# Two token tiles through a chain of feed-forward stages: one more weight unit of distance between the tiles, half of a mean square on VectorE, output stored in halves

## The chip, the cores and the metric

One core of one Trainium2 chip. The metric is the device time of one execution in microseconds; the kernel before has a median of 1438.19 us over 3 runs (1437.05 to 1443.36). PE is the matrix engine (TensorE), PEld its weight load, DVE is VectorE, ACT is ScalarE, POOL is GpSimd, SP issues the transfers.

## What is computed

256 tokens of width 1024 go through two blocks. The first block is a state-space mixer beside a sparse attention, merged, and then a feed-forward with a squared relu (width 4096). The second block has two layers, each with two gated feed-forwards (width 2816) around a mixer (retention in layer 0, latent attention in layer 1):

```python
def swiglu(h, w_gu, w_down):
    g, u = jnp.split(h @ w_gu, 2, axis=-1)
    return (jax.nn.silu(g) * u) @ w_down
...
        x = x + FFN_RES_WEIGHT * rms_norm(swiglu(rms_norm(x, ng[0]), ffn_w_gu[l, 0], ffn_w_down[l, 0]), ng[1])
        h = rms_norm(x, ng[2])
...
        x = x + rms_norm(mix, ng[3])
        x = x + FFN_RES_WEIGHT * rms_norm(swiglu(rms_norm(x, ng[4]), ffn_w_gu[l, 1], ffn_w_down[l, 1]), ng[5])
```

`rms_norm` divides by the root of the mean square over the 1024 columns and multiplies by a gain. So each branch's result is normalised once more before it is added to x; such an addition is called a gained residual below.

## The kernel before

The tokens are two tiles of 128, `t` = 0 and 1. x stays in SBUF, transposed, as `xT[t]` (128 x 8 x 128). Every product is made of three matmuls on values split into a high and a low part: `mm3` (L301) multiplies high by high, low weights by high, and high weights by low. Activations are split into `hTh`/`hTl` or `ffhh`/`ffhl`. Weights arrive in units of up to 128 x 2048 (1 MB) in a buffer `raw`; ACT casts a unit in four pieces to `wh` (L259), and DVE subtracts to get `wl` (L260). A unit is shared by the two tiles: it stays until both have used it, and only then can its buffers be filled again. There are 5 buffers of `wh` and `wl` each and 3 of `raw` in most of the stages here, 6 of `wh` and `wl` in the last one (`XB1`, `XB2`, L175 and L243 to L249).

The stages around the change are these. **f1**: `stage1` (up and down with 8 chunks of 512) and then the first gated feed-forward, ffn00 (11 chunks of 256). Then retention. **f2 of layer 0**: the output product of the mixer (`mix_out`, `wo`), its gained residual, ffn01, and then ffn10. Then latent attention. **f2 of layer 1**: `mix_out`, its gained residual, ffn11, and the output.

In a feed-forward (`ffn`, L423) a chunk's two up-products (12 matmuls for each unit and tile) go to a PSUM tile `mm`, ACT and DVE form `ffh` from it, PE transposes that (`tr`), ACT and DVE split it, and a down-product of 12 matmuls adds it to two accumulators of 512 columns (acc0, acc1 for tile 0; acc2, acc3 for tile 1). Each step of a tile's generator is one weight unit. `drive_gen` (L475) steps the two tiles by turns; tile 1 begins once tile 0 has done more steps than `lag`:

```python
            if alive[0]:
                step(0)
            if alive[1] and (pos[0] > lag or not alive[0]):
                step(1)
```

The default is `self.L`, 1. In f2 the generator of tile 0's `mix_out`, `W`, has already been stepped while the mixer ended, once in layer 0 and twice in layer 1, so tile 0 is there further ahead by that. A scheduler then orders each engine's instructions; what it makes of the steps is shown below as its order.

A residual (`resid`, L389) copies the accumulators to `tsb`, eight transposes on PE bring it back (`tr`), and DVE adds to `xT`. With a gain, ACT takes Square with an accumulated sum over each half (L400), DVE adds the two sums to `ms` (L402), POOL takes the power -1/2 (`rr`, L326), ACT scales the first half (L404) and DVE the second (L405), and DVE adds to `xT` in eight pieces (L420). There are 12 of these: two for ffn00, ffn01, ffn10, ffn11 and each of the two mixers. A stage starts with `norm`: eight pieces of `hTh` (ACT, L379) and `hTl` (DVE, L380), a Square on ACT, a reduction `s` on DVE (L365), and a one-column matmul with `ones`. Where tile 1's residual belongs to the next stage, it is kept in `left` and done there by `flush`.

At the end of `run` the two tiles of `xT` are stored, 512 KB each (L1260).

Of the kernel before, what the change touches and what calls it, by code (L numbers as in the profile page):

```python
# [12 lines left out]
AF = mybir.ActivationFunctionType  # L13
ALU = mybir.AluOpType
PSUM = bass.MemoryType.PSUM
P = 128
UW = 2048
EPS = 1e-6
# [159 lines left out]
class Prog:  # L178
# [207 lines left out]
            self.resid(pool, t, *self.left.pop(t), "sq")  # L386


    def resid(self, pool, t, acc, gain=None, tag=None):  # L389
        nc = self.nc  # L390
        xT = self.xT[t]
        if tag:
            tsb = self.sb(self.np, [P, 8, P], tag).rearrange("p c t -> p (c t)")
        else:
            tsb = self.sb(pool, [P, 1024], f"tsb{t}")
        if gain is not None:
            aa = self.sb(pool, [P, 2], "aa", bufs=4)
            for n in (0, 1):
                j = tsb[:, 512 * n:512 * n + 512]
                nc.scalar.activation(j, acc[n], AF.Square, scale=1.0 / 32.0, accum_out=aa[:, n:n + 1])  # L400
            ms = self.sb(pool, [P, 1], "ms", bufs=4)
            nc.vector.tensor_scalar(ms, aa[:, 0:1], aa[:, 1:2], EPS, op0=ALU.add, op1=ALU.add)  # L402
            r = self.rsqrt(pool, ms, 1, tag="rr")
            nc.scalar.mul(tsb[:, :512], acc[0], r)  # L404
            nc.vector.tensor_scalar_mul(tsb[:, 512:], acc[1], r)  # L405
        else:
            nc.scalar.copy(tsb[:, :512], acc[0])
            nc.vector.tensor_copy(tsb[:, 512:], acc[1])
        for h in (0, 1):
            pt = self.ps("tr")  # L410
            for c in range(4):
                cc = 4 * h + c
                self.tr(pt[:, c * P:(c + 1) * P], tsb[:, cc * P:(cc + 1) * P])
            if gain is None:
                v = xT[:, 4 * h:4 * h + 4, :].rearrange("p c t -> p (c t)")
                nc.vector.tensor_add(v, pt, v)
            else:
                for c in range(4):
                    cc = 4 * h + c
                    nc.vector.scalar_tensor_tensor(xT[:, cc, :], pt[:, c * P:(c + 1) * P], gain[:, cc:cc + 1], xT[:, cc, :], op0=ALU.mult, op1=ALU.add)  # L420


    def ffn(self, pool, t, hT, rstd, up, down, nch, width):  # L423
# [796 lines left out]
    def stage_ffn(self, pool, t, l, i, leave=False):  # L1220
        b = 3 + 6 * l + 4 * i
        h, r = self.norm(pool, t, self.gain(b))
        acc = yield from self.ffn(pool, t, h, r, f"gu{l}{i}", f"fd{l}{i}", 11, 256)
        gh = self.g05[:, 8 * (2 * l + i):8 * (2 * l + i) + 8]
        if leave:
            self.left[t] = (acc, gh)
        else:
            self.resid(pool, t, acc, gh)

    def run(self):  # L1230
        nc = self.nc
        self.consts()
        self.block1_mix()
        for l in (0, 1):
            for i in (0, 1):
                k = 2 * l + i
                nc.vector.tensor_scalar_mul(self.g05[:, 8 * k:8 * k + 8], self.gain(3 + 6 * l + 4 * i + 1), 0.5)
        self.dump("d_x0", self.xT[0])
        es0 = ExitStack()
        self.np = self.ctx.enter_context(self.tc.tile_pool(name="np", bufs=1))  # L1240
        mp = es0.enter_context(self.tc.tile_pool(name="mid", bufs=1))
        with ExitStack() as es:
            pool = es.enter_context(self.tc.tile_pool(name="f1", bufs=1))
            self.xp = es.enter_context(self.tc.tile_pool(name="f1x", bufs=1))
            self.un, self.XB = 0, XB1
            F = self.drive_gen([self.stage1(pool, 0), self.stage1(pool, 1)])
            for _ in range(12):
                next(F)
            D, M = self.decay(pool, mp), self.mem_prep(pool)
            for _ in D:  # L1250
                next(F)
            for _ in M:
                next(F)
            self.weave(F)
            self.xp = None
        self.layer_mix(0)
        es0.close()
        self.layer_mix(1)
        for t in (0, 1):
            nc.sync.dma_start(self.out[t], self.xT[t])  # L1260


    def attention(self, pool, heads, stags, otags):
# [61 lines left out]
    def layer_mix(self, l):  # L1325
        tc = self.tc
        with ExitStack() as es:
            with ExitStack() as es2:
                pool = es2.enter_context(tc.tile_pool(name=f"m{l}", bufs=1))
                self.xp = es2.enter_context(tc.tile_pool(name=f"m{l}x", bufs=1))  # L1330
                self.un, self.XB = 0, XBM[l]
                mix, W = (self.retention if l == 0 else self.mla)(pool)
                self.xp = None
            with ExitStack() as es2:
                pool = es2.enter_context(tc.tile_pool(name=f"f2{l}", bufs=1))

                def tail(t):
                    acc = yield from (W if t == 0 else self.mix_out(t, mix, f"wo{l}"))
                    self.resid(pool, t, acc, self.gain(3 + 6 * l + 3))
                    yield from self.stage_ffn(pool, t, l, 1)  # L1340
                    if l == 0:
                        yield from self.stage_ffn(pool, t, 1, 0, t == 1)

                self.xp = es2.enter_context(tc.tile_pool(name=f"f2{l}x", bufs=1))
                self.un, self.XB = 0, XB2[l]
                F = self.drive_gen([tail(0), tail(1)])
                if l == 0:
                    for _ in range(16):
                        next(F)
                    self.weave(F, self.mem_prep(pool))  # L1350
                self.weave(F)
                self.xp = None
# [277 lines left out]
```

## Time and profile before

| | |
|---|---|
| median of 3 runs | 1438.19 us |
| profiled execution | 1435.33 us, its span 1433.6 us |
| PE busy | 1383.9 us (97%) |
| PEld, DVE, ACT, POOL busy | 1111.8, 925.5, 754.2, 145.5 us |
| memory traffic | mean 166 GB/s |

The busy time of PE is counted from pipelined matmuls, so a busy PE is not a PE at its peak; a start-to-start distance of matmuls tells its pace. The feed-forward stages lie in the span as follows: stage1 from about 246 us, ffn00 from 438, f2 of layer 0 from 755 to about 1145 with ffn10 from 954, f2 of layer 1 from 1230 to the end. The granted clock is 1.00 (the upper of the two levels) in all slices of these stages but the last.

### The profile page before, as it was taken

The page shows a single profiled execution, that of the slowest core. Times are in us where ns is not written, and L with a number is a line of the kernel's source. Part 1 is how long each engine was busy: PE and PEld are TensorE (multiplying, and loading weights), DVE is VectorE, ACT ScalarE, POOL GpSimd, SP SyncE. Part 2 cuts the span into 40 slices and gives each one's busy share as a digit, 9 for nine tenths or more (in the row PEclk, how much of TensorE's full clock was granted, in tenths as well). Part 3 has the DMA queues.
Part 4 walks back from the last instruction along what each step waited for, and adds up shares of the span by engine and source line. Part 5 has one row for each costly group of instructions (what it writes and reads, how often), then busy time and mean ns, then how long its engine had stood idle before and what let it go on. Part 6 is the DMA issues. An engine that isn't in the chain of part 4 may idle for free.

```text
span 1433.6 us, 18512 instructions
## 1 busy us (share of the span) xinstructions
PE 1383.9 (97%) x6706; PEld 1111.8 (78%) x6706; DVE 925.5 (65%) x1970; ACT 754.2 (53%) x1650; POOL 145.5 (10%) x175
## 2 busy tenths in 40 slices
PE   7799899999999999999999999999999999999997
PEld 3466688788887888889887888878888887788886
DVE  6587667955667555577588565576555596765553
ACT  3246555644566444455367464465444576754442
POOL 3655200710000000012000000000000000000000
PEclk9899999999999999999999999999999999999999
DMA  9122255655564555435444555545555252555540
GB/s 345 67 89 78 89 178 176 244 200 176 177 209 170 179 180 195 147 100 191 142 172 168 197 210 179 198 153 206 176 190 192 78 182 78 185 206 186 195 147 30
DMA packets 38828, 238.64 MB, mean 166 GB/s; under 512 B 5712, under 2 KB 6992, under 8 KB 13136
## 3 DMA queue, kind: packets, MB, share of 16 engines
q1 hardware_dynamic: 38736, 237.45, 47.3%
q8 instruction: 53, 0.87, 0.2%
q14 instruction: 39, 0.32, 0.1%
HBM read 236.39 MB, written 1.05 MB: 166 GB/s over the span
## 4 chain that ended last, share of the span: by engine, by line
PE 77%; DVE 9%; POOL 5%; issue 4%; DMA 3%; ACT 2%; SPq 0%; POOLq 0%; DVEq 0%; ACTq 0%
PE mm L219 44%; PE acc L219 29%; PE tr L223 3%; DVE wl L260 2%; DMA raw<-in_wts_dram 2%; DVE s L365 1%; DVE hTl L380 1%; DVE xT L420 1%; POOL cst L719 1%; POOL cst L717 1%; PE tr L219 1%; DMA wl<-in_wts_dram 1%; ACT wh L259 1%; DVE tb L749 0%; POOL X L753 0%
## 5 line engine op out<-in xcount | busy, mean ns | idle before, releaser
L260 DVE TENSOR_TENSOR wl<-raw,wh 128x512 fp32r<-128x512 f32 (+2 forms) x860 | 539.9, 678 | 258.5 <-ACT wh L259 248.5
L259 ACT CAST wh<-raw 128x512 fp32r<-128x512 f32 (+2 forms) x860 | 466.2, 607 | 308.0 <-PE mm L219 158.7
L219 PE MATMUL mm<-wh,hTh 128*128 128x512 f32 (+1 forms) x1040 | 405.1, 390 | 8.5 <-DVE yn L1088 4.6
L219 PE MATMUL mm<-wh,hTl 128*128 128x512 f32 (+2 forms) x1072 | 412.3, 389 | 0.7 <-DVE hTl L380 0.7
L219 PE MATMUL mm<-wl,hTh 128*128 128x512 f32 (+1 forms) x1040 | 399.9, 385 | 0.0
L219 PEld LDWEIGHTS mm<-wh,hTl 128*128 128x128 f32 x1072 | 201.6, 188 | 44.5 <-issue 4.7
L219 PEld LDWEIGHTS mm<-wh,hTh 128*128 128x128 f32 x1040 | 195.7, 188 | 51.0 <-ACT hTh L379 5.8
L219 PEld LDWEIGHTS mm<-wl,hTh 128*128 128x128 f32 x1040 | 195.8, 188 | 37.0 <-issue 0.7
L219 PE MATMUL acc<-wh,ffhh 128*128 128x512 f32 x480 | 196.4, 409 | 0.0
L219 PE MATMUL acc<-wh,ffhl 128*128 128x512 f32 x480 | 188.9, 393 | 0.0
L219 PE MATMUL acc<-wl,ffhh 128*128 128x512 f32 x480 | 188.7, 393 | 0.0
L437 ACT ACTIVATE ffs<-mm,rstd 128x256 f32<-128x256 f32 x88 | 41.7, 474 | 135.8 <-PE mm L219 134.6
L438 DVE SCALAR_TENSOR_TENSOR ffh<-mm,rstd,ffs 128x256 f32<-128x256 f32 x88 | 42.4, 482 | 107.7 <-ACT ffs L437 105.7
L219 PEld LDWEIGHTS acc<-wh,ffhl 128*128 128x128 f32 x480 | 90.2, 188 | 20.2
L219 PEld LDWEIGHTS acc<-wl,ffhh 128*128 128x128 f32 x480 | 90.6, 189 | 16.8
L219 PEld LDWEIGHTS acc<-wh,ffhh 128*128 128x128 f32 x480 | 90.3, 188 | 16.5
L326 POOL TENSOR_TENSOR rr<-ms,mhalf 128x1 f32<-128x1 f32 x12 | 7.1, 595 | 780.5 <-DVE ms L402 780.5
L219 PE MATMUL acc<-wh,mx 128*128 128x512 f32 x160 | 53.9, 403 | 0.2 <-ACT wh L259 0.2
L319 ACT CAST ffhh<-tr 128x256 fp32r<-128x256 f32 (+1 forms) x104 | 41.7, 401 | 21.0 <-PE tr L223 21.0
L320 DVE TENSOR_TENSOR ffhl<-tr,ffhh 128x256 fp32r<-128x256 f32 (+1 forms) x104 | 47.6, 458 | 6.3 <-ACT ffhh L319 5.5
L223 PE MATMUL tr<-idn,ffh 128*128 128x128 f32 x240 | 43.2, 272 | 0.0
L223 PEld LDWEIGHTS tr<-idn,ffh 128*128 128x128 f32 x240 | 32.3, 140 | 13.3 <-DVE ffh L438 0.4
(403 smaller groups left out, 1372.2 us busy)
## 6 DMA issues: line engine op xcount, KB each, us to landing
raw<-in_wts_dram SPq DMA_DIRECT2D x195, 1024.0 KB, 4.9
raw<-in_wts_dram SPq DMA_DIRECT2D x18, 768.0 KB, 4.2
raw<-in_wts_dram SPq DMA_DIRECT2D x4, 576.0 KB, 3.5
wl<-in_wts_dram SPq DMA_DIRECT2D x2, 1024.0 KB, 6.8
g8k<-in_cw_dram SPq DMA_DIRECT2D x2, 1024.0 KB, 10.0
memT<-in_memT_dram SPq DMA_DIRECT2D x4, 512.0 KB, 4.1
raw<-in_wts_dram SPq DMA_DIRECT2D x4, 256.0 KB, 5.3
wh<-in_wts_dram SPq DMA_DIRECT2D x4, 256.0 KB, 7.4
```

The lines of the kernel that those rows point to most:

```text
L219: self.nc.tensor.matmul(out, l, r, start=start, stop=stop, **kw)
L223: self.nc.tensor.transpose(out, src, self.idn[:n, :n])
L259: self.copies[key] = nc.scalar.copy(wh[:, s:s + h], raw[:, s:s + h]).ins
L260: self.subs[key] = nc.vector.tensor_sub(wl[:, s:s + h], raw[:, s:s + h], wh[:, s:s + h].bitcast(F32)).ins
L319: self.nc.scalar.copy(hi, src)
L320: self.nc.vector.tensor_sub(lo, src, hi.bitcast(F32))
L365: nc.vector.tensor_reduce(s8, sq.rearrange("p c t -> p t c"), axis=mybir.AxisListType.X, op=ALU.add)
L380: nc.vector.scalar_tensor_tensor(lo[:, c, :], xT[:, c, :], g[:, c:c + 1], hi[:, c, :].bitcast(F32), op0=ALU.mult, op1=ALU.subtract)
L420: nc.vector.scalar_tensor_tensor(xT[:, cc, :], pt[:, c * P:(c + 1) * P], gain[:, cc:cc + 1], xT[:, cc, :], op0=ALU.mult, op1=ALU.add)
L437: nc.scalar.activation(s, pm[:, :256], AF.Silu, scale=rstd)
L438: nc.vector.scalar_tensor_tensor(h, pm[:, 256:], rstd, s, op0=ALU.mult, op1=ALU.mult)
L717: e.tensor_mul(C[n], A[0], B[n])
```

## The change

Three things are changed. The two drivers of feed-forward stages (f1 and f2) get a lag of 2 in place of 1. In a gained residual, ACT takes Square of the first half only; the second half's mean square is made on DVE from its mean and variance (`bn_stats`, `bn_aggr`, mean squared plus variance, halved, plus epsilon, plus the other half's sum). And in the last residual of each tile the four pieces of `xT` of each half are stored as soon as they are updated, 256 KB each, in place of the two stores at the end.

```diff
-    def resid(self, pool, t, acc, gain=None, tag=None):
+    def resid(self, pool, t, acc, gain=None, tag=None, out=False):
...
             aa = self.sb(pool, [P, 2], "aa", bufs=4)
-            for n in (0, 1):
-                j = tsb[:, 512 * n:512 * n + 512]
-                nc.scalar.activation(j, acc[n], AF.Square, scale=1.0 / 32.0, accum_out=aa[:, n:n + 1])
+            nc.scalar.activation(tsb[:, :512], acc[0], AF.Square, scale=1.0 / 32.0, accum_out=aa[:, 0:1])
+
+            bs, mv = self.sb(pool, [P, 6], "rbs", bufs=2), self.sb(pool, [P, 2], "rmv", bufs=2)
+            nc.vector.bn_stats(bs, acc[1])
+            nc.vector.bn_aggr(mv, bs)
             ms = self.sb(pool, [P, 1], "ms", bufs=4)
-            nc.vector.tensor_scalar(ms, aa[:, 0:1], aa[:, 1:2], EPS, op0=ALU.add, op1=ALU.add)
+            nc.vector.scalar_tensor_tensor(ms, mv[:, 0:1], mv[:, 0:1], mv[:, 1:2], op0=ALU.mult, op1=ALU.add)
+            nc.vector.tensor_scalar(ms, ms, 0.5, EPS, op0=ALU.mult, op1=ALU.add)
+            nc.vector.tensor_add(ms, ms, aa[:, 0:1])
             r = self.rsqrt(pool, ms, 1, tag="rr")
...
                     nc.vector.scalar_tensor_tensor(xT[:, cc, :], pt[:, c * P:(c + 1) * P], gain[:, cc:cc + 1], xT[:, cc, :], op0=ALU.mult, op1=ALU.add)
+                if out:
+                    nc.sync.dma_start(self.out[t][:, 4 * h:4 * h + 4], xT[:, 4 * h:4 * h + 4])
...
-            self.resid(pool, t, acc, gh)
+            self.resid(pool, t, acc, gh, out=l == 1 and i == 1)
...
-            F = self.drive_gen([self.stage1(pool, 0), self.stage1(pool, 1)])
+            F = self.drive_gen([self.stage1(pool, 0), self.stage1(pool, 1)], 2)
...
-        for t in (0, 1):
-            nc.sync.dma_start(self.out[t], self.xT[t])
...
-                F = self.drive_gen([tail(0), tail(1)])
+                F = self.drive_gen([tail(0), tail(1)], 2)
```

The order on the engines shows what becomes of it. First PE between `stage1` and ffn00, from the transposes of tile 1's residual on (`tsb1`; `hTh0` and `hTh1` are the two tiles' activations, and the first number behind a name counts its buffers). Before:

```order
L223 MATMUL tr_687_3878<-idn_1_67,tsb1_686_3875 128x128 x4
L223 MATMUL tr_688_3884<-idn_1_67,tsb1_686_3875 128x128 x4
L219 MATMUL mm_698_3920<-wh_681_3816,hTh1_689_3890 128x512
L219 MATMUL mm_698_3920<-wl_682_3817,hTh1_689_3890 128x512
L219 MATMUL mm_704_3944<-wh_706_3946,hTh0_670_3784 128x512
```

With the change:

```order
L223 MATMUL tr_696_3914<-idn_1_67,tsb1_695_3911 128x128 x4
L223 MATMUL tr_697_3920<-idn_1_67,tsb1_695_3911 128x128 x4
L219 MATMUL mm_691_3886<-wh_709_3970,hTh0_670_3772 128x512
L219 MATMUL mm_691_3886<-wl_710_3971,hTh0_670_3772 128x512
L219 MATMUL mm_691_3886<-wh_709_3970,hTl0_671_3773 128x512
L219 MATMUL mm_691_3886<-wh_709_3970,hTh0_670_3772 128x512
L219 MATMUL mm_707_3956<-wh_681_3804,hTh1_698_3926 128x512
```

Four matmuls of tile 0 now stand between the transposes and the first matmul of tile 1, whose operand `hTh1` is made from what those transposes bring; the 12 matmuls of tile 0's unit before that now stand ahead of the transposes.

Second, ACT in the middle of ffn11, between the casts of weight units (`wh`), the activations `ffs` and the splits `ffhh`. Before:

```order
L259 CAST wh_2077_11885<-raw_2076_11884 128x512 x4
L319 CAST ffhh_2069_11830<-tr_2068_11827 128x256
L259 CAST wh_2085_11932<-raw_2084_11931 128x512 x4
L259 CAST wh_2094_11980<-raw_2093_11979 128x512 x4
L437 ACTIVATE ffs_2080_11921<-mm_2071_11846,rstd01_1915_10908 128x256
L437 ACTIVATE ffs_2088_11956<-mm_2075_11871,rstd11_1949_11111 128x256
L319 CAST ffhh_2082_11927<-tr_2081_11924 128x256
```

With the change:

```order
L259 CAST wh_2117_12054<-raw_2116_12053 128x512 x4
L319 CAST ffhh_2114_12037<-tr_2113_12034 128x256
L259 CAST wh_2126_12102<-raw_2125_12101 128x512 x4
L443 ACTIVATE ffs_2121_12091<-mm_2107_12005,rstd01_1931_10939 128x256
L259 CAST wh_2130_12139<-raw_2129_12138 128x512
L319 CAST ffhh_2123_12097<-tr_2122_12094 128x256
L259 CAST wh_2130_12139<-raw_2129_12138 128x512 x3
```

The activations of the two tiles no longer follow each other; one unit's casts now stand between them, and one of its casts ahead of a split.

Third, DVE at the end of the program, from the last split on. Before:

```order
L320 TENSOR_TENSOR ffhl_2169_12459<-tr_2167_12455,ffhh_2168_12458 128x256
L402 TENSOR_SCALAR ms_2172_12490<-aa_2171_12487 128x1
L405 TENSOR_SCALAR tsb1_2170_12486<-acc3_1951_11114,rr1_2173_12492 128x512
L420 SCALAR_TENSOR_TENSOR xT1_6_79<-tr_2174_12496,g05_10_95,xT1_6_79 128x128 x4
L420 SCALAR_TENSOR_TENSOR xT1_6_79<-tr_2175_12505,g05_10_95,xT1_6_79 128x128 x4
```

With the change:

```order
L320 TENSOR_TENSOR ffhl_2191_12516<-tr_2189_12512,ffhh_2190_12515 128x256
L401 BN_STATS rbs_2194_12546<-acc3_1979_11199 128x6
L402 BN_AGGR rmv_2195_12547<-rbs_2194_12546 128x2
L404 SCALAR_TENSOR_TENSOR ms_2196_12550<-rmv_2195_12547 128x1
L405 TENSOR_SCALAR ms_2196_12550<-ms_2196_12550 128x1
L406 TENSOR_TENSOR ms_2196_12550<-ms_2196_12550,aa_2193_12544 128x1
L409 TENSOR_SCALAR tsb1_2192_12543<-acc3_1979_11199,rr1_2197_12554 128x512
L424 SCALAR_TENSOR_TENSOR xT1_6_79<-tr_2198_12558,g05_10_95,xT1_6_79 128x128 x4
L424 SCALAR_TENSOR_TENSOR xT1_6_79<-tr_2199_12568,g05_10_95,xT1_6_79 128x128 x4
```

Five operations stand where one stood ahead of the scaling by `rr`. In the order of the matmuls as a whole, ffn00 had 24 up-matmuls, 12 down-matmuls, 24 and 12 in turn and now has 48, 12 and 12; ffn11 had 48, 12 and 12 and now has 24, 12, 24 and 12; ffn01 and ffn10 have 48, 12 and 12 in both.

## Rows read from the trace of the kernel before

**Rows 1.** The page: span, then busy time, share and instructions of each engine.

```profile
span 1433.6 us, 18512 instructions
PE 1383.9 (97%) x6706; PEld 1111.8 (78%) x6706; DVE 925.5 (65%) x1970; ACT 754.2 (53%) x1650; POOL 145.5 (10%) x175
```

**Rows 2.** Busy time by stretch: PE, PEld, DVE, ACT, POOL, clock, DMA share, GB/s.

```profile
245.00:262.00 17.00, 15.01 (x73) 11.83 (x72) 16.90 (x30) 12.99 (x27) 1.82 (x2) 1.00 0.53 182
...
430.00:455.00 25.00, 22.77 (x108) 17.89 (x107) 21.31 (x42) 17.86 (x39) 1.48 (x2) 1.00 0.46 164
...
755.00:787.00 32.00, 31.06 (x145) 24.32 (x144) 27.08 (x63) 23.51 (x52) 2.94 (x4) 1.00 0.40 145
...
1230.00:1262.00 32.00, 29.86 (x135) 23.00 (x134) 28.08 (x64) 22.36 (x50) 2.83 (x3) 1.00 0.48 168
1262.00:1400.00 138.00, 138.00 (x625) 113.71 (x624) 74.76 (x132) 65.85 (x132) 0.00 (x0) 1.00 0.52 182
```

**Rows 3.** Waits of PE: what it waited for, us in total, times, longest.

```profile
PE tr L219 <- DVE s L365: 4.3, 10, 0.7
PE tr L223 <- ACT tsb L404: 3.4, 3, 2.4
...
PE mm L219 <- ACT hTh L379: 2.3, 3, 1.3
...
PE mm L219 <- ACT wh L259: 1.0, 1, 1.0
```

**Rows 4.** Timeline of PE at boundaries: start, duration, instruction, idle before and releaser.

```profile
252.44 0.50 PE L219 MATMUL mm<-wh,hTh 128*128 128x512 f32 x1 [0.78 <-ACT hTh L379]
...
443.13 0.50 PE L219 MATMUL mm<-wh,hTh 128*128 128x512 f32 x1 [1.32 <-ACT hTh L379]
...
758.49 1.09 PE L223 MATMUL tr<-idn,tsb 128*128 128x128 f32 x8 [0.66 <-ACT tsb L404]
...
1243.56 0.50 PE L219 MATMUL mm<-wh,hTh 128*128 128x512 f32 x1 [1.01 <-ACT wh L259]
```

**Rows 5.** The chain that ended last, in ffn00 and in ffn11: start, us, what.

```profile
478.49 5.52 PE mm L219 x24
484.01 0.22 PE tr L223 x2
484.23 2.79 PE acc L219 x12
...
1291.93 10.88 PE mm L219 x48
...
1303.03 2.75 PE acc L219 x12
```

**Rows 6.** Instructions by form: busy us, mean ns, idle before and releasers.

```profile
L260 DVE TENSOR_TENSOR wl<-raw,wh 128x512 fp32r<-128x512 f32 x772 | 493.5, 691 | 239.6 <-ACT wh L259 229.6 <-PE mm L219 9.1 <-issue 0.2
L259 ACT CAST wh<-raw 128x512 fp32r<-128x512 f32 x772 | 428.1, 619 | 276.2 <-PE mm L219 141.3 <-PE acc L219 121.2 <-DMA raw<-in_wts_dram 7.2
...
L1278 DVE TENSOR_REDUCE amn<-mm 128x2 f32<-128x512 f32 x10 | 6.9, 685 | 0.8 <-PE mm L219 0.8
...
L1460 DVE BATCH_NORM_STATS2 bs<-acc 128x6 f32<-128x128 f32 x12 | 3.1, 274 | 2.5 <-PE acc L219 2.5
...
L402 DVE TENSOR_SCALAR ms<-aa 128x1 f32<-128x1 f32 x12 | 2.5, 211 | 14.6 <-ACT tsb L400 14.6
...
L1461 DVE BATCH_NORM_AGGREGATE mvs<-bs 128x2 f32<-128x6 f32 x12 | 1.8, 166 | 0.0
```

**Rows 7.** Timeline of the last microseconds.

```profile
1424.29 0.39 PE L219 MATMUL acc<-wh,ffhl 128*128 128x512 f32 x1
...
1425.43 0.21 DVE L402 TENSOR_SCALAR ms<-aa 128x1 f32<-128x1 f32 x1 [4.24 <-ACT tsb L400]
...
1427.73 2.16 DVE L420 SCALAR_TENSOR_TENSOR xT<-tr,g,xT 128x128 f32<-128x128 f32 x8 [0.68 <-PE tr L223]
```

**Rows 8.** The page: transfers issued, KB each, us to landing.

```profile
out_dram<-xT SPq DMA_DIRECT2D x2, 512.0 KB, 2.6
```

## The prediction

> **What bounds the kernel now.** I read the page's busy shares first, then the table of engines by stage, then PE's waits, then PE's own timeline at the stage boundaries, and last the chain inside the feed-forward loops. The shares say that PE is the bound: 1383.9 of 1433.6 us [rows 1]. The profiled execution took 1435.33 us, 2.9 us (0.2%) less than the median of the runs shown, 1438.19; the sum below is made against the profiled one and then carried to the median. By stage [rows 2] the middle of a feed-forward loop has no gap at all (138.00 of 138.00 us), while the four places where a loop begins or gives way to the next lose 2.0 (17 - 15.01), 2.2, 0.9 and 2.1 us. At the same places DVE is nearly full (16.90 of 17, 21.31 of 25, 27.08 of 32, 28.08 of 32 us). PE's waits [rows 3] name what it stands for there: the sum over squares `s` (4.3 us in ten pieces), the transposed rows `hTh`, and `tsb`, whose 3.4 us include 2.4 us at the very end. The timeline puts places to them [rows 4]. So the change can win at most some 8 us at boundaries, plus what a loop's own pace and the last microseconds give; about 0.5%, or 7.2 us, is what a measurement of this kernel can tell from no change.
>
> **The lag: what it removes.** With one more unit of tile 0 ahead, PE's order holds matmuls of tile 0 behind tile 1's transposes, where now it goes straight on to tile 1, whose `hTh` isn't ready. Those waits are 0.78 us in the first stage and 1.32 us between the two feed-forwards of f1 [rows 4]. At the two entries of f2 PE waits for `tsb`, 3.4 - 2.4 = 1.0 us in two pieces [rows 3] of which the first is 0.66, and 1.01 us for a cast of weights [rows 4], and there too more of tile 0's work now stands around the waits. Sum: 0.78 + 1.32 + 1.0 + 1.01 = 4.1 us. The bounds are 0 (each wait only moves to the next operand) and 4.1. I take all of it, since 12 matmuls of cover are 12 x 10.88 / 48 = 2.7 us [rows 5], more than any of these waits. The ten waits for `s` I leave at 4.3 us: they stand where the one-column matmul stands in PE's order, right behind work of its own tile, and the order moves them little.
>
> **The lag: what it adds.** A weight buffer can be refilled only when tile 1 has used it, so a tile 0 that is further ahead shortens the time between a buffer's release and its next use. Counted in the order of the matmuls, that is in f1 some 72 matmuls before and 48 now, in f2 48 before and 24 now, or 5.4 us at that pace. A conversion is four casts of 0.619 us and one trailing subtraction of 0.691 us [rows 6]: 4 x 0.619 + 0.691 = 3.2 us. In the loops that still leaves 2.2 us, and I cost it at nothing; its cover is PE's 24 matmuls, and if ACT's queue eats the 2.2 us the second rival's price falls due. At five places where a stage of f2 starts, the order leaves only 12 to 16 matmuls, 2.7 us and a little more, between release and use: 3.2 - 2.7 = 0.45 us late, five times, 2.2 us. The bounds are 0 (where casts overlap, or the buffer was free earlier) and 3.4 us (1.2 us more at f1's entry, where tile 0's fourth unit must now be loaded and cast earlier). I take 2.2.
>
> **The pace of the loops.** Inside ffn00 24 up-matmuls take 5.52 us and 12 down-matmuls 2.79, so 72 take 2 x 5.52 + 2 x 2.79 + 2 x 0.22 = 17.1 us; in ffn11, whose order is 48 and then 12 and 12, they take 10.88 + 2 x 2.75 + 2 x 0.22 = 16.8 us [rows 5]. Two small transposes, 0.22 us, stand with each 12 down-matmuls. The new order gives ffn00 the pattern of 48, and gives ffn11 the pattern of 24 and 12; ffn01 and ffn10 keep theirs with the tiles exchanged. If the pattern makes the pace, that is 10 cycles x 0.25 = 2.5 us won in ffn00 and 2.5 us lost in ffn11; if something else of f1 makes it, neither happens. Either way I take 0, with plus and minus 2.5 us as bounds, should only one of the two hold.
>
> **The mean square.** Each of the 12 gained residuals loses one ACT Square and its accumulator read, and DVE gets five small or middling operations for one. No row shows the statistics over 512 columns. Below they cost no less than over 128 columns, 0.27 us; the nearest row of that width, a reduction of 512 PSUM columns, takes 0.685 us, and I take that [rows 6]. With the aggregation, 0.17 us, and three small operations at the present one's 0.21 us that is 0.69 + 0.17 + 0.63 = 1.5 us on DVE, 1.3 more than now; between 1.1 and 1.5 by the bounds. Eleven times of twelve PE has matmuls of the other tile meanwhile, so I cost it at nothing there; the third rival is that cover gone. The twelfth is at the end [rows 7]: the last accumulator is done at 1424.29 + 0.39 = 1424.68, and today's `ms` is done at 1425.43 + 0.21 = 1425.64. The new chain would end at 1424.68 + 1.49 = 1426.17: 0.5 us later (0.1 with the short statistics).
>
> On this the Trainium skill speaks against the change: "VectorE: DVE Perf Modes", section "Rules for kernel authors", says of chained VectorE operations that their number is what to keep small, and this edit puts five where one was. The trace agrees that small ones are dear (0.21 us for one column); by that rule alone the third rival's sum below would be the one to take.
>
> **The halves of the output.** After the last update of xT, which ends at 1427.73 + 2.16 = 1429.89 [rows 7], 3.7 us pass until the span ends, most of them the 512 KB transfer's 2.6 us to landing [rows 8]. Now only 256 KB is left at that time. If the bytes made all of those 2.6 us, half of them would save 1.3; if a fixed part made them all, 0. No row here separates the two, so I take the middle, 0.7, and keep 0 and 1.3 as bounds. SP issues four transfers for two, but behind them stands nothing else, and every weight load is ahead of them in SP's order, so no load waits.
>
> **Sum:** -4.1 + 2.2 + 0.5 - 0.7 + 0 = -2.1 us: 1433.2 for an execution like the profiled one, and 1438.19 - 2.1 = **1436.1** for the median. Its own bounds: with every term at its best -4.1 + 0 + 0.1 - 1.3 - 2.5 = -7.8 us (1430.4), at its worst, half of the waits staying, -2.0 + 3.4 + 0.5 + 0 + 2.5 = +4.4 us (1442.6).
>
> **Rivals.**
> First, the lead clears the boundaries altogether: the waits for `s` go too, 4.3 + 2.3 + 1.0 + 1.0 = 8.6 us, the end's 2.4 us taken off [rows 3], with nothing lost at the short covers. With the tail's -0.2 that is -8.8 us, 1429.4, and 1426.9 if ffn00 also wins its 2.5. For it: in the middle of the loops the same instructions are fully covered. Against it: DVE does the reduction of `s`, and it has no spare time at f1's entry. Chance 0.20.
>
> Second, on the other side: **the buffers run short in f2's loops.** The order of ACT shows casts of consecutive units in a row, with the activations between; if another unit's four casts, 2.5 us, stand ahead when a buffer comes free, the conversion ends 2.48 + 3.17 = 5.65 us after the release, 0.2 us too late for 24 matmuls. For one unit of three, 33 units, this costs 33 x 0.21 = 6.9 us; for all 99 units 20.8 us: 1443 to 1457, with 1450 the middle. It decides from 2.2 us of queue on ACT at the release. Against it: ACT is busy for 65.85 of 138.00 us and DVE for 74.76 in such a loop [rows 2], and PE's order frees buffers one at a time. Chance 0.11.
> The Trainium skill, "Perfetto Trace Analysis", section "Optimization Strategy", takes a gap that repeats on the engine that should be full as a sign of too few buffers. The loops before show no such gap, as the 138.00 of 138.00 says; by that rule it is what this rival would look like.
>
> Third, also slower: the mean square lands on a DVE that is full where it matters. Ten of the twelve residuals lie at boundaries; 10 x 1.3 us = 13 us if each one delays the `s` or `tsb` that PE waits for; with that, the sum is -2.1 + 13 = +11, 1449. It needs a DVE that still works off its queue when the second accumulator is complete. Against it: before `ms` DVE stood idle for ACT's Square for 14.6 us in all [rows 6], so DVE has mostly waited for ACT at this step and not the other way round. Chance 0.06.
>
> Fourth, nothing moves: each wait only changes place, and the tail's two edits cancel, 1438. That the lag isn't really raised is excluded, since the order shows tile 0's third unit moved. Chance 0.15. My forecast keeps 0.48.
>
> **The numbers.** Faster by over 0.5% means 1431.0 or less: the first rival (0.20) and the best edge of the forecast (0.03), so 0.23. Slower by over 0.5% means 1445.4 or more: the third rival and most of the second, 0.15. The rest, 0.62, is within. The range reaches from the first rival's better figure, 1427, to 1443.5, a little over the forecast's worst; about 0.17 lies outside, nearly all above.
>
> **What would show it.** Right, if PE's waits for `hTh` and for `tsb` at f2's entries are gone, if small waits on `wh` or `wl` of about half a microsecond stand at the starts of f2's stages, and if ffn11's middle keeps 100% of PE. Wrong, if PE waits on `wh` or `wl` inside the loops, if the waits for `s` go or grow as a group, or if the span of ffn00 or ffn11 changes by over 2.5 us. At the end, `rr` should come 0.5 us later after the last matmul and the span should end 0.7 us sooner after the last update.

## The result: 0.84% slower, and the profile after

The changed kernel takes 1450.92 us (median of 5 runs, 1448.53 to 1455.99) where the kernel before took 1438.19. The ratio is 1.0084 with a 95% interval from 1.0066 to 1.0102: 12.1 us more, between 9.5 and 14.7. Forecast were 1436.1 us and a range up to 1443.5, so the result lies outside it and on the other side of no change. The profiled execution of the changed kernel took 1448.71 us.

The page of the changed kernel, span and shares, against [rows 1]:

```profile
span 1446.9 us, 18554 instructions
PE 1396.9 (97%) x6706; PEld 1114.1 (77%) x6706; DVE 941.9 (65%) x2018; ACT 748.1 (52%) x1626; POOL 146.2 (10%) x175
```

The span grew by 13.3 us and PE's busy time by 13.0. The number of matmuls is the same. Most of the loss is not waiting: the matmuls themselves stand further apart. PE's waits (what it waited for, us in total, times, longest) tell of the smaller part, against [rows 3]:

```profile
PE tr L223 <- ACT tsb L408: 6.2, 9, 3.1
PE tr L219 <- DVE s L365: 4.9, 10, 0.7
...
PE mm L219 <- ACT hTh L379: 1.8, 2, 1.4
PE mm L219 <- DVE hTl L380: 1.6, 3, 0.8
...
PE mm L219 <- DVE wl L260: 0.2, 1, 0.2
```

The wait for `tsb` went from 3 pieces to 9. `hTh` fell from 2.3 to 1.8 us, but `hTl` rose from 0.7 to 1.6, and a wait for the weights hardly exists. Added up over the timeline from 244 us to the end, PE's gaps were 14.05 us before and are 17.68 us now: 3.6 us of the loss. Another 2.0 us lie ahead of 245 us, where no instruction was changed. And the 4224 matmuls of 512 columns from there to the end, counted from start to start without the gaps, took 987.1 us and now take 994.5. These 7.4 us are the largest part.

That part shows in the chain that ended last, here in ffn11 of the changed kernel (start, us, what), against the lower part of [rows 5]:

```profile
1280.23 5.58 PE mm L219 x24
...
1288.83 5.53 PE mm L219 x24
...
1297.35 5.44 PE mm L219 x24
...
1305.77 5.52 PE mm L219 x24
...
1314.28 5.58 PE mm L219 x24
```

Before, 48 up-matmuls took 10.88 us, which is 5.44 for 24. Now only each fourth piece of 24 is that fast. The others are slower by 0.08 to 0.14 us, and after four pieces, 34 us, the same series begins again. A piece is 12 matmuls of each tile, so four pieces use up four units of up-weights, and with the two down-units between them that is one round through the six weight buffers of this stage. So some buffers are slow and some are fast, with PE never idle and the granted clock at 1.00 (130.00 busy of 130.00 us):

```profile
1276.00:1406.00 130.00, 130.00 (x583) 105.98 (x582) 69.92 (x123) 61.54 (x123) 0.00 (x0) 1.00 0.53 186
```

What differs between the buffers is their address. The two new tiles `rbs` and `rmv` of `resid` take 2 x 32 bytes each in the stage's pool, and everything allocated behind them lies 128 bytes higher. The addresses in a partition, as the programs have them:

```
                        before   mod 256     changed   mod 256
hTh0, hTh1 (all)   93920, 102112    224   93920, 102112   224
wh, first three buffers    44768    224       44768       224
wh, f2 layer 1, three more 163040   224      163168        96
wh, f2 layer 0, two more   172256   224      172384        96
ffhh in f2                 144608   224      144736        96
wh, f1, two more           184096    32      184224       160
ffhh in f1                 153440    96      153440        96
```

Here "mod 256" is the remainder of the address after division by 256; each row names the first of its buffers, the others have the same remainder. Before, in f2, weights and activations agreed modulo 256 everywhere. In the changed kernel two of the five buffers of layer 0 and three of the six of layer 1 no longer agree with `hTh`; and since `ffhh` moved too, in the down-products it is the other three buffers that differ. In ffn11 the program's order of matmuls fits the pieces: those of 5.58 us have both their units in moved buffers, those of 5.52 and 5.53 one of two, and those of 5.44 none. That gave the theory to test.

### The profile page after: what moved, and what is told of

The parts are those of the page before. It is cut to its first block, busy times and chain, and to the rows that moved or that the text cites. A ratio compares the mean times of both kernels' runs of the same rounds, so it can differ in the third digit from the quotient of the medians.

```text
span 1446.9 us, 18554 instructions
## 1 busy us (share of the span) xinstructions
PE 1396.9 (97%) x6706; PEld 1114.1 (77%) x6706; DVE 941.9 (65%) x2018; ACT 748.1 (52%) x1626; POOL 146.2 (10%) x175
## 4 chain that ended last, share of the span: by engine, by line
PE 73%; DVE 12%; POOL 5%; issue 4%; DMA 3%; ACT 3%; SPq 0%; POOLq 0%; DVEq 0%; ACTq 0%
PE mm L219 42%; PE acc L219 27%; DVE wl L260 3%; PE tr L223 3%; DMA raw<-in_wts_dram 3%; DVE s L365 2%; DVE hTl L380 1%; DVE xT L424 1%; ACT wh L259 1%; PE tr L219 1%; POOL cst L725 1%; POOL cst L723 1%; POOL cstt L724 0%; DVE tb L755 0%; POOL rr L326 0%
```

## The experiments

Theory A: a matmul is slower when the addresses of its two operands, weights and activations, differ modulo 256, and the change moved them apart by 128. Theory B: the larger distance between the tiles makes the slow pace. Theory C: the mean square on a full DVE makes the loss (the prediction's third rival). The pace given below is the mean distance from one start to the next of 512-column matmuls of a stage, from rows of PE's timeline.

### e1: the lag alone

```diff
-            F = self.drive_gen([self.stage1(pool, 0), self.stage1(pool, 1)])
+            F = self.drive_gen([self.stage1(pool, 0), self.stage1(pool, 1)], 2)
...
-                F = self.drive_gen([tail(0), tail(1)])
+                F = self.drive_gen([tail(0), tail(1)], 2)
```

> The kernel before with the lag of 2 alone; all buffers lie where they lay before. Theory A (the 128 bytes that the new statistics tiles take move the weight buffers against the activations, and matmuls whose two operands differ in address by 128 modulo 256 are slower): the start-to-start distance of the 512-column matmuls in ffn01, ffn10 and ffn11 stays at 227.4 ns, and the time is 1435 to 1441 us. Theory B (the larger distance between the tiles makes the slow pace): 230.2 ns there, 1445 us or more. Theory C (the mean square on a full DVE makes the loss): as before, 1438 us or a little less.

Measured: 1441.4 us, ratio 1.0020 (1.0007 to 1.0032). Pace in ffn01, ffn10, ffn11: 227.4, 227.4, 227.8 ns. Theory B falls. The lag costs 2.9 us by itself (1.0 to 4.6), where the prediction had expected a gain of 1.9.

### e2: the mean square alone

```diff
-            for n in (0, 1):
-                j = tsb[:, 512 * n:512 * n + 512]
-                nc.scalar.activation(j, acc[n], AF.Square, scale=1.0 / 32.0, accum_out=aa[:, n:n + 1])
+            nc.scalar.activation(tsb[:, :512], acc[0], AF.Square, scale=1.0 / 32.0, accum_out=aa[:, 0:1])
+            bs, mv = self.sb(pool, [P, 6], "rbs", bufs=2), self.sb(pool, [P, 2], "rmv", bufs=2)
...
```

> The kernel before with the mean square on DVE alone; its tiles move the buffers by 128 bytes as in the changed kernel. Theory A: 230.2 ns in the loops of f2, time 1445 to 1450 us. Theory B: 227.4 ns, 1438 us. Theory C: 227.4 ns in the loops, the loss at the boundaries, 1445 to 1450 us.

Measured: 1446.61 us, ratio 1.0055 (1.0038 to 1.0071); pace 230.4, 230.0, 230.7 ns. The pace is that of the changed kernel, in loops in which no residual is computed. The buffers move in this kernel as well, so C for the whole loss is not yet excluded; e4 and e9 separate the two.

### e3: the changed kernel with the move made 256 bytes

```diff
-            bs, mv = self.sb(pool, [P, 6], "rbs", bufs=2), self.sb(pool, [P, 2], "rmv", bufs=2)
+            bs, mv = self.sb(pool, [P, 16], "rbs", bufs=2)[:, :6], self.sb(pool, [P, 16], "rmv", bufs=2)[:, :2]
```

> The changed kernel with the two statistics tiles made 64 bytes wide, so that the buffers move by 256 bytes instead of 128. Theory A: 227.4 ns in the loops of f2, time 1437 to 1443 us. Theories B and C: no change from the changed kernel, 1450 us, under B also 230.2 ns.

Measured: 1446.86 us, ratio 1.0054 (1.0037 to 1.0071); pace 227.5, 227.9, 227.9 ns. The pace is back, with the same instructions in nearly the same order. The time came down by 4 us and not to the 1443 that A had as its upper end: 7.8 us of loss (5.3 to 10.2) are something else. The chain in ffn11 of this run:

```profile
1280.58 5.44 PE mm L219 x24
...
1289.01 5.44 PE mm L219 x24
...
1297.44 5.44 PE mm L219 x24
...
1305.86 5.44 PE mm L219 x24
```

Every piece of 24 takes 5.44 us, where the changed kernel has 5.58, 5.53, 5.44 and 5.52. The pattern of 24 and 12, which the prediction had thought might cost 2.5 us, costs nothing.

### e4: the kernel before, moved by 128 bytes

```diff
-            aa = self.sb(pool, [P, 2], "aa", bufs=4)
+            aa = self.sb(pool, [P, 16], "aa", bufs=4)
```

> The kernel before, its operations unchanged; the tile of the partial sums (aa) is made 64 bytes wide, which moves the buffers behind it by 128 bytes. Theory A: 230.2 ns in the loops of f2, 1445 to 1449 us. Theories B and C: 227.4 ns, 1438 us.

Measured: 1444.53 us, ratio 1.0038 (1.0025 to 1.0052); pace 230.3, 230.1, 230.7 ns. No operation changes and nothing is added but 128 bytes of unused space, and the kernel loses 5.5 us (3.6 to 7.5). The chain in ffn11:

```profile
1283.84 11.06 PE mm L219 x48
...
1300.87 11.04 PE mm L219 x48
```

That is 11.04 to 11.06 us against 10.88 of [rows 5]. One cause alone was changed here, the addresses.

### e6: f1 aligned as f2 was

In f1 the prediction had read a pace of 230.0 ns and could not say why. Theory A has a reason: there the two extra weight buffers were 64 bytes off `hTh`, and `ffhh` 128 bytes off most of the weights. This kernel corrects both by unused space.

```diff
+            self.pad(pool, 128)
             self.xp = es.enter_context(self.tc.tile_pool(name="f1x", bufs=1))
             self.un, self.XB = 0, XB1
+            self.pad(self.xp, 64)
```

`pad` allocates a tile of so many bytes for each partition and lets GpSimd clear it once.

> The kernel before with 128 bytes in front of f1's tiles and 64 more in front of its two extra weight buffers, so that activations and weights of f1 have the same address modulo 256, as they have in f2. Theory A in its relative form (what counts is the difference of the two operands' addresses modulo 256): the pace of stage1 and ffn00 falls from 231.7 and 230.0 ns to 227 to 228 ns, 5 us less, 1433 to 1434 us. If addresses matter only in f2, or if f1 is slow for another reason (the squared relu, its orders): pace and time unchanged, 1438 us.

Measured: 1433.64 us, ratio 0.9954 (0.9941 to 0.9968), 6.6 us less within 4.6 to 8.5. The chain in ffn00, against the upper part of [rows 5], where the two figures are 5.52 and 2.79:

```profile
478.52 5.44 PE mm L223 x24
483.97 0.22 PE tr L227 x2
484.19 2.77 PE acc L223 x12
```

Padding alone makes this kernel faster than either. It is also the strongest test of A, since it makes something better that nobody had touched.

### e8, e7 and e12: which differences, and whether the place itself counts

e8 moves everything by the same 32 bytes; e7 and e12 move only the extra weight buffers of f2, by four different distances.

```diff
+        self.pad(cp, 32)
         self.xT = [self.sb(cp, [P, 8, P], f"xT{t}") for t in (0, 1)]
```

> The kernel before with 32 bytes in front of x, so that every buffer behind it moves by 32 bytes and the differences between the operands stay. Relative form of theory A: pace and time unchanged, 227.4 ns and 1438 us. Absolute form (the place within 256 bytes counts for one operand alone): another pace in f2 and a difference of 3 us or more either way.

Measured in e8: 1439.27 us, ratio 1.0002 (0.9991 to 1.0013). This common move does nothing; the relative form holds, as far as a move of 32 bytes can tell.

```diff
                 self.un, self.XB = 0, XB2[l]
+                self.pad(self.xp, (64, 192)[l])
```

> The kernel before with 64 bytes in front of the extra weight buffers of f2 of layer 0, and 192 bytes in that of layer 1; the other three buffers stay. Theory A: the matmuls from the moved buffers slow down by their difference to the activations: about 3 ns of 227 at 64 modulo 256 (from f1 before, where it is 64), and at 192 either the same 3 ns (if it is a distance on a ring) or some other amount. Without an effect of addresses: 227 ns for all.

> The kernel before with 32 bytes in front of the extra weight buffers of f2 of layer 0 and 128 in that of layer 1. From e7 and e4: matmuls from buffers at a difference of 128 take 232.5 to 233.4 ns; at 32 something between 227 and 230 if the cost grows with the distance, more than 230 if a half of 64 bytes is worse.

e12 has `(32, 128)` in the same place. Each of the two was run once, without an interval (1444.56 and 1444.53 us); what they are for is the pace by buffer. For this the rows of PE's timeline were matched with the program's order of matmuls, which names the buffers. The figures are means by stage, without the distances over 0.3 us:

| weights minus activations, modulo 256 | up-matmuls, ns | down-matmuls, ns | from |
|---|---|---|---|
| 0 (all buffers of the stage) | 226.7 to 227.0 | 228.4 to 230.3 | before (f2), e6 (f1 and f2) |
| 32 | 233.5 | 233.5 | e12 |
| 64 | 229.5 to 230.9 | 229.4 to 230.1 | before (f1), changed (f1), e4, e7 |
| 128 | 232.7 to 232.9 | 231.7 to 232.9 | before (f1, down), changed, e4, e12 |
| 192 | 233.1 to 233.4 | 233.1 to 233.5 | before (f1, down), changed (f1, up), e4, e7 |

In stages with buffers of both kinds, the up-matmuls at 0 take 227.1 to 229.7 ns, a little more than alone. The cost does not grow with the distance: 32 is as bad as 192, and 64 the mildest. In the down-products 64 and 0 can't be told apart. So in e12 the second of the two expected forms came true.

### e5: the output in halves alone

```diff
+                if out:
+                    nc.sync.dma_start(self.out[t][:, 4 * h:4 * h + 4], xT[:, 4 * h:4 * h + 4])
...
-        for t in (0, 1):
-            nc.sync.dma_start(self.out[t], self.xT[t])
```

> The kernel before with the output stored in halves alone; no buffer moves. If the last transfer's size sets the end, the time from the last update of xT to the span's end falls from 3.7 us by 0.7 to 0.9 us (the changed kernel shows 2.9), and the time is 1437.5 us. If the halves cost something by themselves, the time is 1439 us or more.

Measured: 1438.61 us, ratio 0.9999 (0.9989 to 1.0009). In its trace the last update of xT ends at 1434.62 and the span at 1437.5, 2.9 us later instead of 3.7, as expected. Over the runs this gain of 0.8 us is within the interval and cannot be told from nothing.

### e9: the mean square alone, without the move

```diff
-            bs, mv = self.sb(pool, [P, 6], "rbs", bufs=2), self.sb(pool, [P, 2], "rmv", bufs=2)
+            bs, mv = self.sb(pool, [P, 16], "rbs", bufs=2)[:, :6], self.sb(pool, [P, 16], "rmv", bufs=2)[:, :2]
```

(on top of e2)

> The mean square on DVE alone, as in the run of it before, but with the statistics tiles 64 bytes wide, so that no difference of addresses changes. Theory A, with the run e4 (6.1 us for the move alone) taken from e2's 8.2 us: 2 us over the kernel before, 1440.5 us, the loops of f2 at 227.4 ns; PE's waits for tsb at the boundaries and at the end 2 to 3 us more than before. If the mean square by itself costs nothing: 1438.5 us. If it is the third rival of the prediction: 1445 us or more.

Measured: 1441.28 us, ratio 1.0015 (1.0003 to 1.0027), 2.2 us (0.4 to 3.9). Its waits for `tsb`:

```profile
PE tr L223 <- ACT tsb L408: 6.1, 8, 3.1
```

2.7 us more than in [rows 3], 0.7 of it at the end (3.1 against 2.4) and 2.0 at the boundaries. So the mean square costs by its own work about 2 us, and theory C explains that much and not more.

### e10: the lag in f2 only

```diff
-                F = self.drive_gen([tail(0), tail(1)])
+                F = self.drive_gen([tail(0), tail(1)], 2)
```

> The lag of 2 in f2 only, f1 as before. By the trace of e1 f1 won 0.8 us and f2 with its neighbours lost 3.5 us: 1442 us. If the loss of e1 came from f1 or from chance: 1438.5 us.

Measured: 1441.56 us, ratio 1.0014 (0.9999 to 1.0028). The loss of the lag is of the size of e1's, but its interval just includes no change; whether f1's part gains is not decided by the times.

### e11: the best version put together

e6, the same padding for the extra weight buffers of the two mixer stages, and the lag of 2 in f1 only:

```diff
+            self.pad(pool, 128)
...
+            self.pad(self.xp, 64)
-            F = self.drive_gen([self.stage1(pool, 0), self.stage1(pool, 1)])
+            F = self.drive_gen([self.stage1(pool, 0), self.stage1(pool, 1)], 2)
...
                 self.un, self.XB = 0, XBM[l]
+                self.pad(self.xp, (192, 160)[l])
```

> The kernel before with the buffers of f1 aligned as in e6, the extra weight buffers of the two mixer stages too, and the lag of 2 in f1 only. From e6 (5.0 us less), e1's 0.8 us in f1, and about 100 matmuls of the mixers at 3 ns: 1438.5 - 5.0 - 0.8 - 0.3 = 1432.4 us. If the lag gives nothing: 1433.5 us, as e6.

Measured: 1431.55 us, ratio 0.9949 (0.9936 to 0.9962), faster than both kernels. Against e6 (0.9954) no difference can be told; nearly all of it is the alignment of f1.

## Why the prediction was wrong

The parts, each run alone, against the kernel before of its own batch:

| part | forecast, us | measured alone, us | interval, us |
|---|---|---|---|
| 128 bytes of move | not in the sum | +5.5 (e4) | 3.6 to 7.5 |
| the lag | -4.1 + 2.2 | +2.9 (e1) | 1.0 to 4.6 |
| the mean square's own work | +0.5 | +2.2 (e9) | 0.4 to 3.9 |
| the halves | -0.7 | -0.1 (e5) | -1.6 to 1.3 |
| sum | -2.1 | +10.5 | |
| the whole change | -2.1 | +12.1 | 9.5 to 14.7 |

**The pace of the loops** is the step that failed. The prediction saw that ffn00 ran at 230 ns and ffn11 at 227, offered the pattern of 24 and 48 or "something else of f1" as causes, and took 0 "either way", with 2.5 us as bounds. The something else was the distance of the operands in memory, and the change altered just that, in f2. Neither the row nor the diff named it. But the diff allocates two new tiles ahead of the weight buffers, and the unexplained difference in pace was in the rows [rows 5]; to bound an unexplained figure by itself was the error, since its cause could be, and was, at work elsewhere. The bound of 2.5 us held for one stage; three stages of f2 paid. In place of the 0 the runs show 5.5 us when the move is added to the kernel before (e4), and 4.3 when it is taken out of the changed kernel (12.1 less e3's 7.8).

**The lag: what it removes.** The two waits for `hTh` in f1, 0.78 and 1.32 us, are gone in the changed kernel, as foreseen. The gain was given back behind them, and the rest of the 4.1 us the lag does not remove: with the lag alone (e1) PE still waits 0.67 us for `tsb` at the first entry of f2, where it was 0.66, and the 1.01 us for `wh` still stand, at 1249.77. PE's gaps from 244 us on add up to 14.05 us before and to 14.73 in e1. In the changed kernel the new ones stand at the following places (PE's timeline):

```profile
785.38 0.50 PE L219 MATMUL mm<-wh,hTl 128*128 128x512 f32 x1 [0.43 <-DVE hTl L380]
...
978.19 0.51 PE L219 MATMUL mm<-wh,hTl 128*128 128x512 f32 x1 [0.43 <-DVE hTl L380]
...
1160.76 0.45 PE L219 MATMUL mm<-wh,hTh 128*128 128x384 f32 x1 [1.40 <-ACT hTh L379]
1162.15 0.45 PE L219 MATMUL mm<-wh,hTl 128*128 128x384 f32 x1 [0.77 <-DVE hTl L380]
```

The largest lie at the entry to latent attention: there the matmul that needs `hTh` comes in PE's order right behind the transposes that its rows wait for. Before, other matmuls stood between, and the one long wait there was 0.75 us for `hTl`. That was the fourth rival, each wait only changes place. It accounts for 0.7 of e1's 2.9 us. Another 0.8 us in e1's trace are the last eight transposes, 1.97 us against 1.18, at a granted clock of 0.72 in those microseconds against 0.83; e8, whose order is the one before, has 1.94 there, so this needs no lag.

Most of what is left in e1's trace lies at that same entry. Behind two waits of PE the granted clock stood at 0.50, the lower of its two levels, for 3.41 us (PE's timeline, then busy time by stretch as in [rows 2]):

```profile
1154.32 0.45 PE L219 MATMUL mm<-wh,hTh 128*128 128x384 f32 x1 [0.83 <-ACT hTh L379]
...
1155.94 0.45 PE L219 MATMUL mm<-wh,hTl 128*128 128x384 f32 x1 [1.00 <-DVE hTl L380]
...
1156.75:1160.16 3.41, 3.41 (x12) 3.41 (x12) 3.30 (x7) 3.38 (x9) 0.32 (x1) 0.50 0.30 123
```

The matmuls of 384 columns there start 0.32 us apart, where those ahead start 0.175 apart; over that stretch this is about 1.5 us. None of the other thirteen traces has such a stretch between 245 us and the last matmul of ffn11, those of e10 and the changed kernel with the same lag included, so it is no fixed price of the lag, and that the waits brought it about is not shown. Of the 2.9 us a part may not be the lag's at all: within each kernel the runs of the record are about 0.8 us longer for each 0.001 of lower mean granted clock, and e1's runs had on average 0.0014 less than those of the kernel before, by that 1.1 us. How much of the 2.9 us is the lag's own stays open.

**The lag: what it adds.** The five short covers were costed at 2.2 us. PE waits for `wl` for 0.2 us in all, and neither e1 nor the changed kernel has a new wait for `wh` at a start of f2's stages. This term is 0, its lower bound. The second rival (buffers short in the loops) didn't occur: 130.00 of 130.00 us busy.

**The mean square.** The end came as worked out. The rows of the last microseconds, against [rows 7]:

```profile
1437.64 0.70 DVE L401 BATCH_NORM_STATS2 rbs<-acc 128x6 f32<-128x512 f32 x1 [3.51 <-PE acc L219]
1438.37 0.18 DVE L402 BATCH_NORM_AGGREGATE rmv<-rbs 128x2 f32<-128x6 f32 x1
1438.59 0.22 DVE L404 SCALAR_TENSOR_TENSOR ms<-rmv 128x1 f32<-128x1 f32 x1
1438.84 0.15 DVE L405 TENSOR_SCALAR ms<-ms 128x1 f32<-128x1 f32 x1
1439.10 0.16 DVE L406 TENSOR_TENSOR ms<-ms,aa 128x1 f32<-128x1 f32 x1
1439.34 0.54 POOL L326 TENSOR_TENSOR rr<-ms,mhalf 128x1 f32<-128x1 f32 x1 [14.93 <-DVE ms L406]
...
1440.65 1.97 PE L223 MATMUL tr<-idn,tsb 128*128 128x128 f32 x8 [3.05 <-ACT tsb L408]
1441.81 2.16 DVE L424 SCALAR_TENSOR_TENSOR xT<-tr,g,xT 128x128 f32<-128x128 f32 x8 [1.14 <-PE tr L223]
```

The statistics over 512 columns take 0.70 us, taken were 0.69. The chain to `rr` is 1.6 us from 1437.64 to 1439.26, taken were 1.5. PE waits 3.05 us where it waited 2.36, so 0.7 longer, forecast 0.5. Its row before was:

```profile
1427.04 1.18 PE L223 MATMUL tr<-idn,tsb 128*128 128x128 f32 x8 [2.36 <-ACT tsb L404]
```

"Eleven times of twelve PE has matmuls of the other tile meanwhile, so I cost it at nothing" was wrong by 2 us: six more boundaries got a wait of 0.2 to 0.6 us for `tsb`. The third rival had the mechanism right and its size wrong by a factor of six. It supposed that each residual pays its whole 1.3 us.

Here the rule that spoke against the change was right in direction. "VectorE: DVE Perf Modes" of the Trainium skill, section "Rules for kernel authors", wants few chained operations; e9 puts 2.2 us on these twelve, against 13 had none of them been covered.

**The halves of the output.** 1446.9 - (1441.81 + 2.16) = 2.9 us from the last update to the end, against 3.7 [rows 7]: 0.8 us, forecast 0.7. Right in the trace, but too small for the times.

**What was left over.** The profiled spans also differ by 2.0 us at 245 us, ahead of any changed instruction; in other profiled executions with the same code up to there it is 1.4 to 6.4 us. The mean granted clock between 32 and 147 us was 0.91 in the profile before, 0.90 in the changed kernel and 0.85 in the two runs that were latest at 245 us. That is why the parts in the table come from the times and not from differences of single spans. And the sum of the parts is 1.6 us under the whole; the intervals allow that, as they do a little more when lag and mean square meet at the same boundaries (e3, with all but the move, has 1.0054, 7.8 us, where its parts have 5.0).

## What to carry to other kernels

A difference in pace between stages that run the same instructions is a finding, and its cause should be looked for before a change is costed, because an edit can carry it elsewhere. Where the matmuls bound the kernel, write down the addresses of both operands, before and after the edit: a new tile of a few bytes moves all that is allocated behind it. Round small tiles up, so that the large buffers keep their distance, and compare the kernels with a padded variant as well before blaming the edit's own work.

## What the chip showed that was not expected

The pace of these fp32r matmuls (128 x 128 weights loaded from the activations, 512 columns streamed from the weight buffers) depends on the difference of the two operands' addresses within 256 bytes: 226.9 ns at 0, 230 at 64, 232.7 at 128, 233.3 at 192, 233.5 at 32. A difference of 256 is as good as 0 (e3, 226.8 to 227.0 ns), and a move of all buffers by 32 bytes changes nothing (1.0002). These are the up-products; the down-products have 228.4 to 230.3 ns at 0 and are as slow as the others at 32, 128 and 192. All buffers of these kernels start at multiples of 32 bytes, and only the five differences above were tried. What in the memory or in the engine makes it so, no run here shows. In PE's busy share nothing of it can be seen: it is 97% in both kernels.
